# A recurrent unit whose weights rotate through five pairs of buffers in place of three

## The chip, the cores and the metric

The kernel runs on one core of a Trainium2 chip. The metric is the time of one execution in microseconds (us), measured on the device. TensorE is called PE, VectorE DVE, ScalarE ACT, GpSimd POOL and SyncE SP, as in the profile.

## What is computed

One inference step of two layers for 640 tokens (512 latent, 128 context) of width 1024: neighbourhood attention and an FFN, then a gated linear recurrent unit and an FFN. The change is in the recurrent unit:

```python
def _lru_mixer(xm, h0, w_in, conv_w, conv_b, w_a, b_a, w_i, b_i, lam, w_out):
    gate, xr = jnp.split(xm @ w_in, 2, axis=-1)
    xc = _centred_depthwise_conv(xr, conv_w, conv_b)             # width 4
    a_f, b_f = _rglru_coeffs(xc, w_a[0], b_a[0], w_i[0], b_i[0], lam[0])
    a_b, b_b = _rglru_coeffs(xc, w_a[1], b_a[1], w_i[1], b_i[1], lam[1])
    hs_f, hT_f = _linear_scan(a_f, b_f, h0[:, 0], reverse=False)
    hs_b, hT_b = _linear_scan(a_b, b_b, h0[:, 1], reverse=True)
    y = (hs_f + hs_b) * jax.nn.gelu(gate)
    return y @ w_out, jnp.stack([hT_f, hT_b], axis=1)
# _rglru_coeffs: r, i = sigmoid(block-diagonal products of xc); a = exp(-8 r softplus(-lam))
#                b = sqrt(1 - a*a) * i * xc
```

## The kernel before

Features lie on the 128 partitions and tokens along the row; a feature block is 128 features, of which there are eight. A matrix product in fp32 is made of three products in a reduced format: a weight tile of 128 x 1024 elements (one output block, 512 KB) is split into a high part and the low rest, the input likewise, and PE does high x high, high x low and low x high (lines L221 to L223).

`unit` loads one such weight tile. SP fetches `raw` (three buffers). In the recurrent stage POOL fetches the same tile a second time straight into the high part `whi` (L178); in the other stages ACT casts it from `raw` (L180). DVE subtracts (`wlo` = `raw` - `whi`, L182). `whi` and `wlo` have three buffers each, so the fourth tile waits until PE has finished with the first. In both FFN stages a second set, `whx` and `wlx`, takes turns with them (tags in the stage's own pool, three buffers each at most); in the recurrent stage all 16 tiles of `w_in` go through the three pairs.

The recurrent stage runs over t = 0 to 9 as a pipeline of four parts for the eight blocks:
- `lru_xr(f)`: product for the branch `xr` in two pieces of 384 and 256 tokens (tiles `mm`), copied out by ACT (L1251).
- `lru_a`: convolution `xc`, a first step on ACT (L1259) and three on DVE (L1261); four gate products on PE (`gp`, L1271, two PSUM buffers), each read by ACT with a tanh (L1272); an elementwise step on DVE (L1273).
- `lru_b`: exponentials, tanh and square root on ACT (L1283 to L1285), DVE steps L1279, L1286, L1287.
- `lru_c`, `lru_d`: scans on DVE (L1296), POOL copies of a last column to `st` (L1298), sums (L1303, L1304), the product with the GeLU gate (L1308) and the split into high and low (ACT L1313, DVE L1315). `lru_gate` makes the gate's product and its GeLU.

The order in which each engine does its instructions is set when the kernel is built: a scheduler with its own model of durations places them, and each engine then works strictly in that order. Number of buffers and code together therefore decide the queues. Around the end of the stage the output product `project_halves` begins, with three output tiles accumulated over blocks 0 to 5 first and over 6 and 7 when these are ready. Its weights (`in_wlo`) are cast by ACT into `whi` and `whx`.

Of the kernel before, what the change touches and what calls it, by code (L numbers as in the profile page):

```python
# [10 lines left out]
F32R = mybir.dt.float32r  # L11
# [4 lines left out]
P = 128  # L16
# [109 lines left out]
class _Step:  # L126
# [33 lines left out]
        return self.t([P, KT, NTOK + 2], dt, "big", 4)[:, :, 0:n]  # L160


    def unit(self, src, slot=None, after=None):
        nc = self.nc
        _, a, b = src.shape
        raw = self.t([P, a, b], F32, "raw", 3)
        nc.sync.dma_start(raw, src)
        if slot is None:
            self.nu += 1
            slot = "x" if self.wx and self.nu % 2 == 0 else "m"  # L170
        if slot == "x":
            hi = self.t([P, a, b], F32R, "whx", 3, self.sb)
            lo = self.t([P, a, b], F32R, "wlx", 3, self.sb)
        else:
            hi = self.t([P, a, b], F32R, "whi", 3)
            lo = self.t([P, a, b], F32R, "wlo", 3)
        if self.ptags == ["at"]:
            nc.gpsimd.dma_start(hi, src)  # L178
        else:
            nc.scalar.copy(hi, raw)  # L180
        with self.tc.issue_after(after) if after else nullcontext():
            nc.vector.tensor_tensor(lo, raw, hi.bitcast(F32), ALU.subtract)  # L182
        return hi, lo
# [1052 lines left out]
        nc.vector.tensor_scalar(self.hb, self.cols[:, c:c + 4 * KT], 0.5, None, ALU.mult)  # L1236

    def halves(self, w, hi, lo, ev, after=None):
        u = self.unit(w, None, after)
        return [lambda t0=t0, t1=t1, **kw: ev(t0, self.chunk(u, hi, lo, t0, t1, **kw)) for t0, t1 in CHL]  # L1240

    def lru_xr(self, f, hi, lo, after=None):
# [95 lines left out]
    def run(self):  # L1338
# [83 lines left out]
        ylo = self.big()  # L1422
        with self.phase("lru", at=1) as lp:
            A, B, C, G = {}, {}, {}, {}
            self.xrs = [self.t([P, 648], F32, f"xr{j}", 1, lp) for j in range(2)]
            for xr in self.xrs:
                for a, b in ((0, 2), (514, 517), (645, 648)):
                    nc.gpsimd.memset(xr[:, a:b], 0.0)

            def gate(g, after=None):  # L1430
                G[g], halves = self.lru_gate(g, xhi, xlo, lp, after)
                return halves
            x0, g0, x1 = self.lru_xr(0, xhi, xlo), gate(0, self.sq), self.lru_xr(1, xhi, xlo, self.dg)
            x0[0](pins={3: self.at})
            g0[0](pins={0: self.rr})
            for step in (x1[0], x0[1], g0[1]):
                step()
            for t in range(KT + 2):
                if t < KT:
                    A[t] = self.lru_a(t, lp)  # L1440
                if t + 1 < KT:
                    for step in self.lru_xr(t + 1, xhi, xlo) if t else x1[1:]:
                        step()
                if 0 < t <= KT:
                    B[t - 1] = self.lru_b(t - 1, *A.pop(t - 1))
                if t > 1:
                    C[t - 2] = self.lru_c(t - 2, *B.pop(t - 2))
                if t > 2:
                    for step in gate(t - 2):
                        step()  # L1450
                if t > 1:
                    self.lru_d(t - 2, C.pop(t - 2), G.pop(t - 2), yhi, ylo)
            nc.gpsimd.dma_start(o["nh"], self.st)
# [34 lines left out]
```

## Time and profile before

| | us |
|---|---|
| median of the runs | 1523.04 (1518.65, 1523.07, 1523.04) |
| profiled execution, time | 1522.37 |
| profiled execution, span | 1520.6 |
| recurrent stage in the span | about 858 to 1024 |
| PE busy | 1491.2 |
| DVE busy | 1061.5 |
| ACT busy | 698.1 |
| POOL busy | 261.4 |

The span is the part between the first and the last instruction of the profile; times in timelines are from its start. Durations of neighbouring instructions overlap somewhat on PE, DVE and ACT, since they are pipelined, so that a step's cost in a solid stretch is the difference of two starts. "Waited for" names the releaser that the profile infers from semaphores.

### The profile page before, as it was taken

How to read it: one execution, taken by the hardware profiler on the slowest of the kernel's cores; microseconds unless marked ns; L12 is line 12 of the kernel's file. 1: busy time of each engine (PE TensorE's matmuls, PEld its weight loads, DVE VectorE, ACT ScalarE, POOL GpSimd, SP SyncE). 2: the span in 40 equal slices, each digit the busy share in tenths (PEclk: the TensorE clock that was granted, in tenths of full speed). 3: DMA queues.
4: the chain of work that ended last, by engine and by line, in shares of the span. 5: the costliest groups of instructions: out<-in, count | busy, mean ns of one | idle time of the engine just before them, and what ended most of it. 6: DMA issues, size and time to landing. Idle time of an engine off the chain costs nothing. (4 is left out here: it accounts for less than half of the span.)

```text
span 1520.6 us, 26116 instructions
## 1 busy us (share of the span) xinstructions
PE 1491.2 (98%) x10373; PEld 1441.8 (95%) x10373; DVE 1061.5 (70%) x2005; ACT 698.1 (46%) x1268; POOL 261.4 (17%) x276
## 2 busy tenths in 40 slices
PE   8999999999999999999999999899999999999997
PEld 5999999889999999999999887799999999999997
DVE  5778998679999997434443769876975655566555
ACT  4676766654332123312321478764644342434243
POOL 0112132100111110000000014230232323222211
PEclk9999999999999999999999999999999999999999
DMA  9644665446556664222222543316242231323211
GB/s 375 174 143 160 186 189 167 117 139 194 176 185 195 207 196 132 62 84 84 65 73 83 150 134 102 119 59 216 70 156 80 74 111 57 100 67 97 71 56 70
DMA packets 72330, 196.65 MB, mean 129 GB/s; under 512 B 8048, under 2 KB 24592, under 8 KB 72080
## 3 DMA queue, kind: packets, MB, share of 16 engines
q1 hardware_dynamic: 57392, 142.32, 29.6%
q0 software_dynamic: 14240, 51.98, 11.1%
q8 instruction: 81, 1.33, 0.4%
q10 hardware_dynamic: 576, 0.68, 0.1%
q14 instruction: 41, 0.34, 0.1%
HBM read 179.48 MB, written 8.92 MB: 124 GB/s over the span
## 5 line engine op out<-in xcount | busy, mean ns | idle before, releaser
L221 PE MATMUL mm<-big,whi 128*128 128x320 f32 (+3 forms) x1233 | 383.9, 313 | 4.0 <-ACT big L1313 2.8
L222 PE MATMUL mm<-big,whi 128*128 128x320 f32 (+3 forms) x1233 | 384.2, 312 | 1.7 <-DVE big L1315 1.3
L223 PE MATMUL mm<-big,wlo 128*128 128x320 f32 (+3 forms) x1233 | 384.1, 312 | 0.2 <-DVE wlo L182 0.2
L221 PEld LDWEIGHTS mm<-big,whi 128*128 128x128 f32 x1233 | 233.0, 189 | 6.7 <-ACT big L1313 3.5
L222 PEld LDWEIGHTS mm<-big,whi 128*128 128x128 f32 x1233 | 233.6, 189 | 3.8 <-DVE big L1315 2.2
L223 PEld LDWEIGHTS mm<-big,wlo 128*128 128x128 f32 x1233 | 233.2, 189 | 1.6 <-DVE wlo L182 0.4
L250 DVE SCALAR_TENSOR_TENSOR mprod<-mraw,csb 128x1024 f32<-128x1024 f32 x160 | 194.9, 1218 | 11.8 <-DMA mraw<-in_wm 11.4
L590 DVE SCALAR_TENSOR_TENSOR x<-mm,G,x 128x320 f32<-128x320 f32 (+2 forms) x192 | 77.8, 435 | 82.4 <-PE mm L223 82.3
L180 ACT CAST whi<-raw 128x1024 fp32r<-128x1024 f32 (+1 forms) x71 | 73.9, 1041 | 113.9 <-PE mm L222 65.6
L182 DVE TENSOR_TENSOR wlo<-raw,whi 128x1024 fp32r<-128x1024 f32 (+1 forms) x87 | 105.9, 1218 | 28.7 <-ACT whi L180 16.5
L221 PE MATMUL mm<-big,whx 128*128 128x320 f32 (+3 forms) x348 | 108.4, 311 | 0.0
L223 PE MATMUL mm<-big,wlx 128*128 128x320 f32 (+3 forms) x348 | 108.0, 310 | 0.0
L222 PE MATMUL mm<-big,whx 128*128 128x320 f32 (+3 forms) x348 | 107.9, 310 | 0.0
L246 POOL DMA_DIRECT2D mraw<-in_wm x80 | 43.0, 537 | 358.6 <-DVE mprod L250 266.0
L221 PE MATMUL mx<-big,whi 128*128 128x320 f32 (+3 forms) x287 | 89.5, 312 | 0.0
L223 PE MATMUL mx<-big,wlo 128*128 128x320 f32 (+3 forms) x287 | 88.9, 310 | 0.0
L222 PE MATMUL mx<-big,whi 128*128 128x320 f32 (+3 forms) x287 | 88.7, 309 | 0.0
L221 PE MATMUL mx<-big,whx 128*128 128x320 f32 (+3 forms) x260 | 80.6, 310 | 0.0
L223 PE MATMUL mx<-big,wlx 128*128 128x320 f32 (+3 forms) x260 | 80.5, 310 | 0.0
L180 ACT CAST whx<-raw 128x1024 fp32r<-128x1024 f32 (+1 forms) x40 | 41.1, 1029 | 85.9 <-PE mm L222 47.3
L222 PE MATMUL mx<-big,whx 128*128 128x320 f32 (+3 forms) x260 | 80.3, 309 | 0.0
L1313 ACT CAST whi<-raw 128x1024 fp32r<-128x1024 f32 (+1 forms) x41 | 41.3, 1008 | 70.3 <-PE mm L222 45.2
(347 smaller groups left out, 3725.3 us busy)
## 6 DMA issues: line engine op xcount, KB each, us to landing
raw<-in_gu SPq DMA_DIRECT2D x88, 512.0 KB, 3.5
mraw<-in_wm POOLq DMA_DIRECT2D x80, 512.0 KB, 3.9
raw<-in_dn SPq DMA_DIRECT2D x24, 512.0 KB, 3.6
sw<-in_wm SPq DMA_DIRECT2D x16, 512.0 KB, 10.7
raw<-in_wqk SPq DMA_DIRECT2D x16, 512.0 KB, 4.8
raw<-in_wi SPq DMA_DIRECT2D x16, 512.0 KB, 3.5
whi<-in_wi POOLq DMA_DIRECT2D x16, 512.0 KB, 3.9
raw<-in_dn SPq DMA_DIRECT2D x16, 448.0 KB, 3.3
```

Of the source, the lines that this page charges most:

```text
L180: nc.scalar.copy(hi, raw)
L182: nc.vector.tensor_tensor(lo, raw, hi.bitcast(F32), ALU.subtract)
L221: nc.tensor.matmul(ps, hi[:, k], xhi[:, k, s], start=(k == 0), stop=False)
L222: nc.tensor.matmul(ps, hi[:, k], xlo[:, k, s], start=False, stop=False)
L223: self.done = nc.tensor.matmul(ps, lo[:, k], xhi[:, k, s], start=False, stop=(k == last)).ins
L246: nc.gpsimd.dma_start(w, self.i["wm"][l * 6 + j - 2, f])
L250: nc.vector.scalar_tensor_tensor(prod, w, 1.0, self.csb[:, s], ALU.mult, ALU.mult, accum_out=out[:, s, f:f + 1])
L590: self.nc.vector.scalar_tensor_tensor(xs, ps[:, a - t0:b - t0], G[:, s, f:f + 1], xs, ALU.mult, ALU.add)
L1313: self.nc.scalar.copy(hi, v)
```

## The change

The tiles of `w_in` are counted (`lu`, 1 to 16 in the order of the calls). Tiles 6, 8, 11, 13 and 16 use a second set, `whx` and `wlx`, with two buffers in the recurrent stage's own pool; the other eleven stay with the three old pairs. Two pairs of 2 x 4 KB per partition are added. The number of `raw` buffers stays three. From line 1239 on, a line of the kernel after reads one higher than before, and from 1426 on two higher.

```diff
-    def unit(self, src, slot=None, after=None):
+    def unit(self, src, slot=None, after=None, nx=3):
...
         if slot == "x":
-            hi = self.t([P, a, b], F32R, "whx", 3, self.sb)
-            lo = self.t([P, a, b], F32R, "wlx", 3, self.sb)
+            hi = self.t([P, a, b], F32R, "whx", nx, self.sb)
+            lo = self.t([P, a, b], F32R, "wlx", nx, self.sb)
...
     def halves(self, w, hi, lo, ev, after=None):
-        u = self.unit(w, None, after)
+        self.lu += 1
+        u = self.unit(w, "x" if self.lu > 4 and self.lu % 5 in (1, 3) else "m", after, 2)
         return [lambda t0=t0, t1=t1, **kw: ev(t0, self.chunk(u, hi, lo, t0, t1, **kw)) for t0, t1 in CHL]
...
         with self.phase("lru", at=1) as lp:
             A, B, C, G = {}, {}, {}, {}
+            self.lu = 0
```

The scheduler places the instructions anew. Three places follow; numbers in names count tiles, so that a name means the same in both kernels (`whx_10793` and `whi_10793` are the same weight tile in another buffer).

POOL in the middle of the stage, before, weight tiles 12 to 16 and the copies of last columns between them:

```order
L1298 COPY st_74<-lt_9826 128x1 x2
L178 DMA whi_10454<-in_wi 128x1024
L1298 COPY st_74<-lt_9933 128x1
L178 DMA whi_10533<-in_wi 128x1024
L1298 COPY st_74<-lt_9933 128x1
L178 DMA whi_10640<-in_wi 128x1024
L1298 COPY st_74<-lt_10100 128x1 x2
L178 DMA whi_10721<-in_wi 128x1024
L178 DMA whi_10793<-in_wi 128x1024
```

The same copies on POOL after:

```order
L1299 COPY st_74<-lt_9826 128x1 x2
L178 DMA whi_10640<-in_wi 128x1024
L1299 COPY st_74<-lt_9933 128x1
L178 DMA whi_10721<-in_wi 128x1024
L1299 COPY st_74<-lt_9933 128x1
L178 DMA whx_10793<-in_wi 128x1024
L1299 COPY st_74<-lt_10100 128x1 x2
```

Each place between two copies holds a weight tile two further on, and none is left behind the copies of `lt_10100`.

DVE at the last block's convolution (`xc_10595`), before; `wlo_10722` is the low part of tile 15:

```order
L1303 TENSOR_TENSOR lt_10345<-lt_10100 128x448
L1279 TENSOR_SCALAR lt_10433<-lt_10433 128x1286
L1304 TENSOR_TENSOR lt_10345<-lt_10100 128x128
L1261 SCALAR_TENSOR_TENSOR xc_10595<-xr_1598_9510,cols_61,xc_10595 128x643 x2
L182 TENSOR_TENSOR wlo_10722<-raw_10719,whi_10721 128x1024
L1261 SCALAR_TENSOR_TENSOR xc_10595<-xr_1598_9510,cols_61,xc_10595 128x643
L1273 SCALAR_TENSOR_TENSOR lt_10434<-lt_10434,xc_10428 128x1286
```

DVE at the same place after; `wlo_10876` is the low part of the first output weight:

```order
L1304 TENSOR_TENSOR lt_10345<-lt_10100 128x448
L1280 TENSOR_SCALAR lt_10433<-lt_10433 128x1286
L1305 TENSOR_TENSOR lt_10345<-lt_10100 128x128
L182 TENSOR_TENSOR wlo_10876<-raw_10873,whi_10875 128x1024
L1262 SCALAR_TENSOR_TENSOR xc_10595<-xr_1598_9510,cols_61,xc_10595 128x643 x3
L1274 SCALAR_TENSOR_TENSOR lt_10434<-lt_10434,xc_10428 128x1286
```

The output weight's subtraction came here from behind the elementwise step of block 7 (`lt_10601`, L1273), and tile 15's went to the place ahead of the convolution of block 6 (`xc_10428`), where tile 13's stood.

ACT near 898 us, before, at the square root of block 0 (`lt_9677`) and the gate products of block 2 (`gp_9827`, `gp_9831`):

```order
L1272 ACTIVATE lt_9825<-gp_9827,l_hb_2016 128x643
L1285 ACT_TABLE_LOAD
L1285 ACTIVATE lt_9677<-lt_9677 128x1286
L1259 ACTIVATE xc_9927<-xr_1598_9510,cols_61 128x643
L1272 ACT_TABLE_LOAD
L1272 ACTIVATE lt_9825<-gp_9831,l_hb_2016 128x643
```

ACT at the same place after:

```order
L1286 ACT_TABLE_LOAD
L1286 ACTIVATE lt_9677<-lt_9677 128x1286
L1273 ACT_TABLE_LOAD
L1273 ACTIVATE lt_9825<-gp_9827,l_hb_2016 128x643
L1260 ACTIVATE xc_9927<-xr_1598_9510,cols_61 128x643
L1273 ACTIVATE lt_9825<-gp_9831,l_hb_2016 128x643
```

The tanh of `gp_9827` moved behind the square root and both table loads, and the first convolution step of block 3 (`xc_9927`) stays behind both.

## Prediction

> **What bounds the kernel now.** I read the page's busy times first, then the waits of TensorE (PE), then the recurrent stage in stretches, then its timelines. The page's line for the engines (busy us, share of the span, instructions):
>
> ```profile
> span 1520.6 us, 26116 instructions
> PE 1491.2 (98%) x10373; PEld 1441.8 (95%) x10373; DVE 1061.5 (70%) x2005; ACT 698.1 (46%) x1268; POOL 261.4 (17%) x276
> ```
>
> PE idles 29 us in the whole execution, and the change removes no matmul, so only PE's waits and its clock can give time back. PE's waits between 840 and 1060 us (total, times, longest):
>
> ```profile
> PE gp L1271 <- ACT lt L1285: 2.2, 1, 2.2
> PE gp L1271 <- ACT lt L1272: 1.9, 1, 1.9
> PE gp L1271 <- DVE xc L1261: 1.7, 1, 1.7
> PE mm L221 <- ACT big L1313: 1.6, 1, 1.6
> PE mm L223 <- DVE wlo L182: 0.2, 1, 0.2
> ```
>
> The direct wait for a weight is 0.2 us. The four larger ones, which I call A (1.9), B (1.7), C (2.2) and the closing wait T (1.6), are for gate products, convolution and outputs, so weight buffers can help only through the queues of the engines that make these. The stage in stretches (busy us of PE, PEld, DVE, ACT, POOL; granted clock; DMA):
>
> ```profile
> 907.00:917.70 10.70, 8.84 (x53) 7.68 (x52) 10.70 (x14) 9.85 (x14) 9.20 (x3) 1.00 0.27 75
> 917.70:921.20 3.50, 3.50 (x10) 2.47 (x10) 3.50 (x5) 1.80 (x3) 3.50 (x1) 0.51 0.45 147
> 921.20:960.00 38.80, 38.68 (x232) 34.09 (x232) 33.33 (x41) 34.97 (x49) 12.21 (x12) 1.00 0.37 116
> 960.00:982.60 22.60, 18.70 (x109) 15.96 (x108) 19.71 (x23) 18.13 (x25) 4.81 (x4) 1.00 0.39 110
> 982.60:986.00 3.40, 3.40 (x10) 2.29 (x9) 3.37 (x4) 1.71 (x3) 0.00 (x0) 0.50 0.52 202
> 986.00:1022.00 36.00, 35.83 (x237) 34.49 (x236) 27.74 (x34) 23.56 (x31) 10.51 (x6) 1.00 0.17 49
> ```
>
> Behind A and behind C PE runs some 3.4 us at half clock, which costs 1.7 us each beside the wait. In 907 to 917.7 DVE never rests; it sets A.
>
> **Wait C.** Timelines around it (start, length, engine, work, in brackets the idle time before):
>
> ```profile
> 974.91 1.81 DVE L1261 SCALAR_TENSOR_TENSOR xc<-xr,cols,xc 128x643 f32<-128x643 f32 x2
> 979.57 1.23 DVE L182 TENSOR_TENSOR wlo<-raw,whi 128x1024 fp32r<-128x1024 f32 x1 [2.85 <-PE mm L223]
> 980.71 0.88 DVE L1261 SCALAR_TENSOR_TENSOR xc<-xr,cols,xc 128x643 f32<-128x643 f32 x1
> 973.05 2.79 POOL L1298 COPY st<-lt 128x1 f32<-128x1 f32 x1 [0.47 <-DVE lt L1296]
> 975.78 0.53 POOL L178 DMA_DIRECT2D whi<-in_wi  x1
> 981.70 3.75 PE L1271 MATMUL gp<-xc,gw 128*128 128x512 f32 x8 [2.16 <-ACT lt L1285]
> whi<-in_wi POOLq DMA_DIRECT2D x16, 512.0 KB, 3.9
> ```
>
> The trace names the square root (L1285) as C's releaser, but PE starts 0.11 us after the third convolution step (980.71 + 0.88), which the products read: that is what it waited for. In DVE's queue the subtraction for whi_10721 stands between the second and the third step; its weight is issued by POOL at 975.78, behind a one-column copy that takes 2.79 us, and lands 3.9 us later, at 979.7. So a weight that PE needs only some 15 us later holds the convolution.
>
> With the change that weight's subtraction stands 20 us earlier, and here stands the one for the first output weight (wlo_10876), cast by ACT with no POOL DMA. The cast needs the buffer that the products of mm_10485 leave, and these end where ACT copies their result:
>
> ```profile
> 970.35 0.49 ACT L1251 COPY xr<-mm 128x128 f32<-128x128 f32 x2 [0.94 <-PE mm L223]
> 999.74 1.04 ACT L180 CAST whi<-raw 128x1024 fp32r<-128x1024 f32 x1
> 983.41 0.80 ACT L1272 ACTIVATE lt<-gp,l_hb 128x643 f32<-128x643 f32 x1 [0.40 <-PE gp L1271]
> ```
>
> The cast runs at 970.4 to 971.4, long before DVE asks at 975.0. DVE then does 1.14 us of subtraction and three steps of 0.9 (1.81 over two): ready near 978.9 where it was 981.59. PE comes at 981.70 - 2.16 = 979.54, so C goes. With it goes, in this execution, the half-clock stretch. Price on ACT: everything behind 970.35 slides by 1.04. It was ready for the next tanh at 983.01 (983.41 less 0.40 idle) and will be near 984.6 with A's slip added; that tanh ends at 985.4, which is when PE's next product would want its bank (982.2 after the two products, plus 18 matmuls of 0.175). No new PE wait over half a microsecond. PE's lead behind C: 2.16 + 1.7 - 0.5 (the slip of A, below) = 3.4 us.
>
> **Wait B stays.** It has the same cause:
>
> ```profile
> 952.16 3.52 POOL L1298 COPY st<-lt 128x1 f32<-128x1 f32 x1 [10.99 <-DVE lt L1296]
> 955.62 0.53 POOL L178 DMA_DIRECT2D whi<-in_wi  x1
> 959.47 1.23 DVE L182 TENSOR_TENSOR wlo<-raw,whi 128x1024 fp32r<-128x1024 f32 x1 [3.83 <-PE mm L223]
> ```
>
> The new order has another weight there (whi_10721 in place of whi_10533), still behind the same copy on POOL and still ahead of the convolution on DVE: the 3.83 us of DVE and the 1.7 us of PE remain. Gain 0.
>
> **Wait A grows.** ACT takes a tanh out of its place: before, it ran ahead of a square root, now behind it and behind two table loads.
>
> ```profile
> 898.08 0.79 ACT L1272 ACTIVATE lt<-gp,l_hb 128x643 f32<-128x643 f32 x1
> 898.89 1.28 ACT L1285 ACT_TABLE_LOAD   x1
> 900.18 1.28 ACT L1285 ACTIVATE lt<-lt 128x1286 f32<-128x1286 f32 x1
> 902.91 0.88 DVE L1261 SCALAR_TENSOR_TENSOR xc<-xr,cols,xc 128x643 f32<-128x643 f32 x1
> 917.48 2.29 PE L1271 MATMUL gp<-xc,gw 128*128 128x512 f32 x4 [1.86 <-ACT lt L1272]
> ```
>
> Load, root and load from 898.09 end at 902.0, the tanh at 902.7, and the convolution's first step on ACT (0.9) at 903.6; DVE takes it up 0.7 us later than 902.91. DVE has no rest until 917.7 to absorb that, so A's end slips by 0.7; two more matmuls now stand ahead of it (0.24). Net +0.45. One ACT table load more in the stage (22 for 21) falls into the gap that ACT has behind 917.43 and is hidden. In 921 to 960 PE waits 0.12 us of 38.8, DVE and ACT rest 5.5 and 3.8: the slip is carried, not grown. DVE also waits longer for whi_10454 near 926 (up to 1.6 where it waited 0.4); the 1.2 us that it rests at 932 take that up.
>
> **Early weights.** Two extra pairs cost two POOL issues at 852 and 863, and their subtractions move to 863 and 878. PE waits for nothing in 860 to 900, so they cost nothing while whi_9751 (issued behind them) still lands by 871. Subtractions, casts and bytes keep their number.
>
> **The close.** What ends the stage is the chain through the last two outputs, not PE:
>
> ```profile
> 990.04 0.80 ACT L1272 ACTIVATE lt<-gp,l_hb 128x643 f32<-128x643 f32 x1 [2.60 <-PE gp L1271]
> 1004.20 2.45 ACT L1285 ACTIVATE lt<-lt 128x1286 f32<-128x1286 f32 x2
> 1019.00 1.21 DVE L182 TENSOR_TENSOR wlo<-raw,whi 128x1024 fp32r<-128x1024 f32 x1
> 1023.69 1.46 ACT L1313 CAST big<-lt 128x640 fp32r<-128x640 f32 x2 [10.99 <-DVE lt L1308]
> 1024.47 0.41 PE L221 MATMUL mm<-big,whi 128*128 128x320 f32 x1 [1.57 <-ACT big L1313]
> ```
>
> The tanh at 990.04 waits for PE; with PE 3.4 earlier it runs at 986.9, behind two other ACT steps: 3.2 gained. The exponentials then wait some 0.7 for DVE, which now does an output's low part ahead of the scans: the roots come 2.45 earlier than 1004.20. From there DVE is solid, and the subtraction at 1019.00 (1.14 net of overlap) has moved out of that stretch: the cast comes 3.6 earlier. PE, 3.4 earlier, still waits 1.4 for it. In the last pass PE's matmuls now stand tile by tile and no longer interleaved by what is ready: two waits of about 0.2 more for low parts. Gain at the stage's end 3.2 us; behind it PE is solid, and the gain is kept.
>
> **Sum.** C's wait and half clock -3.85; A +0.45; the close +0.2: -3.2. The profiled execution took 1522.37 us, the median of the runs is 1523.04, 0.67 above it. So 1519.2 for an execution like the profiled one, **1519.8** against the median.
>
> **A rule weighed.** The gap of 2.16 us is followed by a clock of 0.50, the gap of 1.86 by 0.51, while the gaps of 1.7 (B) and 1.6 (T) are followed by 1.00. The Trainium skill (TensorE: Matmul & The Clock Gate, Why this matters for your kernels) says that gaps between matmuls should stay under about 3 us, a window of idleness being what halves the clock. By that rule no gap here costs clock and the sum would be -1.5, 1521.5; the trace does not agree, two gaps of about 2 us did cost it. The same page (Part 1) has the window free-running, which no single execution here can show.
>
> **Rivals.**
> 1. The half clock is chance. Gaps of 1.6 and 1.7 us went free, those of 1.9 and 2.2 did not, and one run shown is 4.4 us below the other two, about 2.6 such costs. If the runs of before mostly had no half clock behind C, only 3.2 - 1.7 = 1.5 us are gained: 1521.5.
> 2. More goes: B too, if the copy on POOL happens to get through early. Then 1.7 more, or A's half clock is missed: 1518.1.
> 3. The change does not do what it says: the cast or the table loads ahead of the last convolution come so late that C stays. That needs 978.9 to become 981.6, 2.7 us of slip on ACT or DVE. A's +0.45 and the +0.2 of the last pass would be left, less the 1.14 at the close: -0.5, 1522.5.
> 4. Slower: the weight that DVE now wants near 914.7 (whx_10366) is issued between two copies on POOL:
>
> ```profile
> 908.40 1.00 POOL L1298 COPY st<-lt 128x1 f32<-128x1 f32 x1 [12.88 <-DVE lt L1296]
> 910.03 12.52 POOL L1298 COPY st<-lt 128x1 f32<-128x1 f32 x1
> 906.65 1.28 DVE L1296 TENSOR_TENSOR_SCAN lt<-lt,cols,lt 128x512 f32<-128x512 f32 x1
> ```
>
> The first copy fits into the scans (1.00 us); the second missed them and took 12.52. If A's slip of 0.7 lets the first miss them too, it frees itself only when DVE stops at 914.7; the weight then lands at 914.7 + 0.2 + 3.9 = 918.8, DVE loses 4.1 us where it is the bound, and PE most of that and a further half clock: 5.8 - 3.2 = +2.6, 1525.6. It decides if the first copy starts less than its 1.0 us ahead of the scans' end; I see 1.2.
>
> By the Trainium skill (GPSIMD Engine Reference, Key points) POOL contends with DVE instructions that read two inputs from SBUF, as scans do; then the first copy would be held as well and rival 4 would be the forecast, 1525.6. The row of 1.00 inside the scans speaks against it.
>
> **Chances.** Forecast 0.45 (within 1517.8 to 1521.3), rival 1 0.20, rival 2 0.15, rival 3 0.11, rival 4 0.09. About 0.3% (4.6 us) is what a measurement can tell from no change. Faster by more, below 1518.5: rival 2's most, and the forecast's lower part (0.45 x 0.45), 0.34. Slower by more, above 1527.6: rival 4 together with C staying, 0.08. The rest, 0.58. The range leaves out the far ends of rivals 2 and 4: 1516.0 to 1523.8.
>
> **What would show it.** Right: no PE wait at about 980 and clock 1.00 in the 6 us behind it; the DVE wait of about 3.8 us ahead of 960 and B still there; A between 2 and 2.5 us; a wait at the stage's end of 1 to 1.5 us for the cast. Wrong: a PE wait over 1 us between 978 and 990 (rival 3), DVE idle some 4 us near 915 (rival 4), half clock in a new place, or PE waiting for a weight near 871.

## The result, and the profile after

The changed kernel took 1524.17 us (median of 12 runs, 1518.21 to 1525.75) beside 1521.32 us of the kernel before (12 runs): ratio 1.0026, 95% interval 1.0014 to 1.0037. The forecast was 1519.8, with a range up to 1523.8. A second comparison gave 1523.66 beside 1520.37, ratio 1.0012, 0.9995 to 1.0029. (The ratios compare whole sets of runs and not the two medians, so they can differ from the quotient of the medians.) So by the first comparison the change costs 0.1 to 0.4%, where some 0.2% were to be gained; the second agrees with that, but does not exclude that it costs nothing. The profiled execution of the changed kernel took 1525.75 us, 1.6 over its median.

The page's span and engines after, and two stretches (busy us of PE, PEld, DVE, ACT, POOL; granted clock; DMA):

```profile
span 1524.0 us, 26113 instructions
PE 1492.0 (98%) x10373; PEld 1442.6 (95%) x10373; DVE 1062.5 (70%) x2005; ACT 699.0 (46%) x1269; POOL 264.0 (17%) x276
968.33:971.75 3.42, 3.10 (x5) 1.61 (x6) 3.42 (x4) 1.95 (x4) 0.00 (x0) 0.50 0.00 0
971.75:985.00 13.25, 13.25 (x81) 11.40 (x80) 11.06 (x15) 11.60 (x16) 4.15 (x2) 1.00 0.26 81
```

PE's timeline after, the rows of the recurrent stage ahead of which PE was idle (start, length, work, in brackets the idle time before and its releaser):

```profile
903.44 1.35 PE L1272 MATMUL gp<-xc,gw 128*128 128x512 f32 x4 [0.78 <-ACT lt L1273]
918.72 1.35 PE L1272 MATMUL gp<-xc,gw 128*128 128x512 f32 x4 [1.88 <-ACT lt L1273]
933.04 1.35 PE L1272 MATMUL gp<-xc,gw 128*128 128x512 f32 x4 [1.23 <-ACT lt L1273]
946.26 2.40 PE L1272 MATMUL gp<-xc,gw 128*128 128x512 f32 x8 [0.32 <-issue]
968.65 3.95 PE L1272 MATMUL gp<-xc,gw 128*128 128x512 f32 x8 [3.30 <-DVE xc L1262]
1003.50 0.44 PE L221 MATMUL mm<-big,whx 128*128 128x384 f32 x1 [0.44 <-ACT gl L1326]
1024.33 0.41 PE L221 MATMUL mm<-big,whi 128*128 128x320 f32 x1 [0.73 <-ACT big L1314]
1025.19 0.41 PE L222 MATMUL mm<-big,whi 128*128 128x320 f32 x1 [0.45 <-DVE big L1316]
```

C is gone: no wait near 980, and the clock is 1.00 from 971.75 to 985. But B, which was to stay at 1.74, is 3.30 and has a half-clock stretch of its own at 968.33, and there are new waits at 903, 933 and 946. Measured between the same matmuls of PE, the stage from 842 to 1048 us took 0.16 us less than before: what C and the half clock behind A, absent this time, gave, B with its half clock and the new waits took back.

The 3.4 us between the two profiled spans lie elsewhere. Up to the stage the changed kernel was 0.58 us behind, from half-clock stretches near the start, and between 1085 and 1130 it lost 2.75 more. There a weight landed late (waits of that part, before first, then after):

```profile
ACT wuh L1313 <- DMA raw<-in_gu: 0.8, 1, 0.8
ACT wuh L1314 <- DMA raw<-in_gu: 2.0, 1, 2.0
PE mm L1142 <- DVE g L1104: 1.8, 1, 1.8
```

PE waited 1.8 us where it had waited 0.5, with one more half-clock stretch. No instruction of that part changed its place, and the same wait was 1.58 and 1.30 us in two more profiles of the kernel before, and 1.16 and 1.32 us in two more of the changed kernel. The 0.5 us was the exception: this is chance, and one pair of profiles does not tell what the change did.

### The profile page after: what moved, and what is told of

Same layout as the page of the kernel before. It is cut to its first block, busy times and chain, and to the rows that moved or that the text cites. A ratio compares the mean times of both kernels' runs of the same rounds, so it can differ in the third digit from the quotient of the medians.

```text
span 1524.0 us, 26113 instructions
## 1 busy us (share of the span) xinstructions
PE 1492.0 (98%) x10373; PEld 1442.6 (95%) x10373; DVE 1062.5 (70%) x2005; ACT 699.0 (46%) x1269; POOL 264.0 (17%) x276
## 5 line engine op out<-in xcount | busy, mean ns | idle before, releaser
L221 PE MATMUL mm<-big,whi 128*128 128x320 f32 (+3 forms) x1153 | 358.6, 313 | 3.0 <-ACT big L1314 2.0
L222 PE MATMUL mm<-big,whi 128*128 128x320 f32 (+3 forms) x1153 | 358.8, 312 | 2.0 <-DVE big L1316 1.8
L223 PE MATMUL mm<-big,wlo 128*128 128x320 f32 (+3 forms) x1153 | 358.1, 312 | 0.0
L221 PEld LDWEIGHTS mm<-big,whi 128*128 128x128 f32 x1153 | 217.5, 189 | 5.6 <-ACT big L1314 2.7
L222 PEld LDWEIGHTS mm<-big,whi 128*128 128x128 f32 x1153 | 218.2, 189 | 4.1 <-DVE big L1316 2.4
L223 PEld LDWEIGHTS mm<-big,wlo 128*128 128x128 f32 x1153 | 217.6, 189 | 1.0
L221 PE MATMUL mm<-big,whx 128*128 128x320 f32 (+3 forms) x428 | 133.7, 312 | 0.5 <-ACT gl L1326 0.4
L223 PE MATMUL mm<-big,wlx 128*128 128x320 f32 (+3 forms) x428 | 133.1, 311 | 0.0
L222 PE MATMUL mm<-big,whx 128*128 128x320 f32 (+3 forms) x428 | 132.8, 310 | 0.0
L180 ACT CAST whi<-raw 128x1024 fp32r<-128x1024 f32 (+1 forms) x71 | 73.9, 1040 | 114.5 <-PE mm L222 66.4
L221 PEld LDWEIGHTS mm<-big,whx 128*128 128x128 f32 x428 | 80.6, 188 | 1.1 <-ACT gl L1326 0.7
L222 PEld LDWEIGHTS mm<-big,whx 128*128 128x128 f32 x428 | 80.9, 189 | 0.0
L223 PEld LDWEIGHTS mm<-big,wlx 128*128 128x128 f32 x428 | 80.7, 188 | 0.0
L221 PE MATMUL mx<-big,whx 128*128 128x320 f32 (+3 forms) x260 | 80.6, 310 | 0.0
```

The costliest lines, as they stand in the source:

```text
L221: nc.tensor.matmul(ps, hi[:, k], xhi[:, k, s], start=(k == 0), stop=False)
L222: nc.tensor.matmul(ps, hi[:, k], xlo[:, k, s], start=False, stop=False)
L223: self.done = nc.tensor.matmul(ps, lo[:, k], xhi[:, k, s], start=False, stop=(k == last)).ins
```

## The experiments

The first theory, P, came from POOL's and DVE's timelines after, around 911 to 962:

```profile
911.20 12.66 POOL L1299 COPY st<-lt 128x1 f32<-128x1 f32 x1
923.80 0.53 POOL L178 DMA_DIRECT2D whi<-in_wi  x1
927.75 1.23 DVE L182 TENSOR_TENSOR wlo<-raw,whi 128x1024 fp32r<-128x1024 f32 x1 [1.60 <-issue]
938.49 11.27 POOL L1299 COPY st<-lt 128x1 f32<-128x1 f32 x2 [7.37 <-ACT lt L1284]
949.70 0.53 POOL L178 DMA_DIRECT2D whi<-in_wi  x1
953.65 1.23 DVE L182 TENSOR_TENSOR wlo<-raw,whi 128x1024 fp32r<-128x1024 f32 x1 [3.94 <-issue]
957.25 1.02 POOL L1299 COPY st<-lt 128x1 f32<-128x1 f32 x1 [7.03 <-DVE lt L1297]
958.22 0.53 POOL L178 DMA_DIRECT2D whi<-in_wi  x1
962.16 1.23 DVE L182 TENSOR_TENSOR wlo<-raw,whi 128x1024 fp32r<-128x1024 f32 x1 [1.39 <-issue]
```

The three weights are whi_10454, whi_10640 and whi_10721. The second copy of block 2 (`lt_9826`; 9.78 of the 11.27 us) ended when DVE came to rest at 949.7, and DVE rested because it wanted whi_10640, which POOL issues behind that copy: each held the other. The next copy then came later, and with it whi_10721. Two rivals: Q, that the order on ACT and DVE makes the waits whatever POOL does; R, that the loss is chance outside the stage.

**The changed kernel again**, unaltered.

> The changed kernel once more, unaltered, timed and profiled again. Theory P (the copies hold POOL's queue): with the change the weight of tile 14 (whi_10640) came to stand behind the second copy of the last state of block 2, which took 9.78 us where its counterpart took 1.03; VectorE waited 3.94 us and then 1.39 us for weights and wait B grew from 1.74 to 3.27 us. It is fixed by the order, so it comes again: a copy of 9 to 10 us near 940, B at 3.1 to 3.4 us, ratio to the kernel before 1.0015 to 1.0035. Rival R (chance outside the stage): in the profiled pair the stage itself took 0.16 us less than before and the loss of 2.75 us lay at 1090 to 1115, behind one weight that landed 1.2 us late. Then that place is back at a wait of 0.5 us, and the ratio is 0.9995 to 1.001.

Measured: 1523.66 us (1515.63 to 1525.45, 12 runs). Its profile is of an execution of 1515.63 us (POOL, then PE):

```profile
908.59 6.75 POOL L1299 COPY st<-lt 128x1 f32<-128x1 f32 x1
935.85 3.20 POOL L1299 COPY st<-lt 128x1 f32<-128x1 f32 x1 [0.47 <-DVE lt L1297]
900.83 1.35 PE L1272 MATMUL gp<-xc,gw 128*128 128x512 f32 x4 [0.78 <-ACT lt L1273]
916.13 2.14 PE L1272 MATMUL gp<-xc,gw 128*128 128x512 f32 x4 [1.89 <-ACT lt L1273]
```

The same program, and the two copies took 6.75 and 3.20 us in place of 12.66 and 9.78. B is gone; the stage took 4.5 us less than in the first profile of before. The waits at 933 and 946 are absent too, but for another reason: here a half clock follows A, and PE, some 1.7 us later from there on, meets its products ready. The stretch behind A and the one that follows it, in this profile and then in the first one after:

```profile
916.50:919.90 3.40, 3.40 (x9) 2.09 (x8) 3.40 (x5) 3.35 (x6) 0.00 (x0) 0.51 0.62 190
919.90:960.00 40.10, 40.10 (x242) 36.02 (x241) 37.62 (x45) 36.38 (x48) 13.54 (x10) 1.00 0.43 119
918.70:922.10 3.40, 3.38 (x15) 2.43 (x16) 3.40 (x4) 3.37 (x5) 3.40 (x1) 1.00 0.16 66
922.10:960.00 37.90, 36.35 (x219) 32.03 (x218) 32.37 (x40) 33.96 (x47) 18.22 (x11) 1.00 0.37 106
```

P had said that B is fixed by the order: wrong, the copies' lengths differ between executions of one program, in an order that stays the same. R was wrong as well, since the stage itself differs by 4.3 us between two executions. What the 25 timed executions of the changed kernel show fits that: 5 at 1515.6 to 1518.8, 20 at 1521.1 to 1525.8, none between. The 87 of the kernel before, in this comparison and the later ones, have no such gap (33 below 1519, 24 from 1519 to 1521, 30 above).

**The copies on VectorE**, first in the changed kernel, then in the one before.

```diff
-            nc.gpsimd.tensor_copy(st, h[:, d, e:e + 1])
+            nc.vector.tensor_copy(st, h[:, d, e:e + 1])
```

> The changed kernel with the 16 one-column copies of the last states on VectorE in place of POOL, so that nothing stands ahead of a weight on POOL's queue. Theory P: VectorE's waits for weights near 950 and 961 (3.94 and 1.39 us) fall below 0.5 us together, B falls from 3.27 to under 1 us, and the time falls by 2.3 to 5 us against the changed kernel: ratio to before 0.9985 to 1.0008. Rival Q (the growth comes from ScalarE's order, a tanh behind a square root and one more table load, and from the order on VectorE): B stays above 2.5 us, ratio 1.0015 to 1.003.

> The kernel before with the same copies on VectorE, and three pairs of buffers as it had. Theory P: waits B (1.74 us) and C (2.16 us) both came from weights behind these copies and go; with them goes a half-clock stretch of 1.7 us where it followed C: 3.5 to 5.6 us less, ratio 0.9963 to 0.998. Rival Q (the buffers come free too late, whatever stands on POOL): B and C stay above 1.4 us each, ratio 0.9995 to 1.0005.

Measured: 1524.77 us, ratio 1.0031 (1.0019 to 1.0043), and 1525.73 us, ratio 1.0033 (1.0019 to 1.0047). Both slower, against P. PE's longest wait in the stage, of each:

```profile
PE mm L221 <- ACT big L1314: 6.0, 1, 6.0
PE mm L221 <- ACT big L1313: 8.0, 1, 8.0
```

B and C are at 0.83 us or less in both, as P says, but a wait of 6 to 8 us for the last output's cast stands at the stage's end, with 6.8 us of half clock. Beside the copies themselves the edit moved some two dozen or more instructions each on DVE and ACT and over 150 matmuls on PE, so these two runs mix two changes. They do not decide.

**Two early pairs alone.**

```diff
-        u = self.unit(w, "x" if self.lu > 4 and self.lu % 5 in (1, 3) else "m", after, 2)
+        u = self.unit(w, "x" if self.lu in (6, 8) else "m", after, 2)
```

> Only tiles 6 and 8 take the extra pairs; 11, 13 and 16 go back to the three main pairs. The tanh behind the square root near 902 belongs to this half, the weights of the second half again change their places among POOL's copies. Theory P: the early half costs under 0.7 us by itself, and the time is decided by the copies ahead of tiles 12 to 15 near 940 to 980; ratio 0.999 to 1.0015. Rival Q (ScalarE's order): A at 1.9 to 2.5 us and the new waits of 0.8 and 1.2 us near 903 and 930 come with it, ratio 1.0015 to 1.003.

Measured: 1523.37 us, ratio 1.0016 (1.0001 to 1.003), just inside Q's range and just above P's, with an interval that reaches into both. Its profile has the 0.77 us near 903, so that wait belongs to the early half; it has waits of 2.41 and 2.15 us for a tanh near 932 and 991, the second in no other kernel: another order again. Inconclusive on the time.

**The states by a DMA on POOL's own queue**: now the weights stand behind an issue that does not copy. For the changed kernel the order on PE, ACT, DVE and SP is the same, instruction for instruction; for the one before, one convolution step on DVE moves.

```diff
-            nc.gpsimd.tensor_copy(st, h[:, d, e:e + 1])
+            nc.gpsimd.dma_start(st, h[:, d, e:e + 1])
```

> The changed kernel with the 16 last states written by a DMA on POOL's queue in place of a POOL copy; the order on every other engine is the same, instruction for instruction. Theory P2 (a lottery): the second copy of a pair is starved by VectorE for 1 to 12.7 us, differently in each execution of the same program (12.66 us and 6.75 us for the same copy in two profiles of the changed kernel), and decides whether wait B is 0 or 3.3 us; the changed kernel's executions fall into a group at 1515 to 1519 us and a larger one at 1521 to 1526 for that reason. Without copies the slow group goes: median 1515 to 1518.5, B below 0.5 us, no wait near 934, ratio to before 0.9965 to 0.999. Rival Q (order on ScalarE and VectorE): two groups as before, median 1522 to 1525, ratio 1.001 to 1.003.

> The same edit on the kernel before (one convolution step on VectorE moves, all else keeps its order). P2: B (1.74 us) and C (2.16 us) go, with one half-clock stretch: median 1515 to 1518.5, ratio 0.996 to 0.999. If the two kernels then differ, that is what the buffers alone are worth: P2 says within 1.5 us of one another. Rival Q: B and C stay, ratio 0.9995 to 1.0005, and the changed kernel with this edit is 2 to 4 us slower than this one.

Measured: 1517.15 us (1515.25 to 1521.51), ratio 0.9991 (0.998 to 1.0002), and 1517.59 us (1516.23 to 1518.91), ratio 0.9988 (0.9978 to 0.9998). POOL's rows in the changed kernel with this edit, where the copies of blocks 0 and 2 had been, then DVE's first wait for a weight behind 900, then PE's waits in the stage for a tanh and at the close (total, times, longest):

```profile
910.33 0.54 POOL L1299 DMA_DIRECT2D st<-lt  x1 [0.41 <-issue]
937.49 0.53 POOL L1299 DMA_DIRECT2D st<-lt  x1 [0.96 <-ACT lt L1285]
955.13 1.22 DVE L182 TENSOR_TENSOR wlo<-raw,whi 128x1024 fp32r<-128x1024 f32 x1 [1.24 <-issue]
PE gp L1272 <- ACT lt L1273: 2.6, 2, 1.9
PE mm L221 <- ACT big L1314: 0.7, 1, 0.7
```

No state takes over 0.55 us, B is gone, and but for one run at 1521.51 none is above 1519.9. By the medians that is 6.5 to 7 us less than the changed kernel, which was timed in other comparisons; by the ratios to the kernel before, each within its own comparison, it is 3 to 5 us less. In the kernel before the same edit takes C away and leaves 0.49 of B, in a profile without a half clock behind A:

```profile
963.53 1.78 PE L1271 MATMUL gp<-xc,gw 128*128 128x512 f32 x5 [0.49 <-DVE xc L1261]
PE mm L221 <- ACT big L1313: 1.6, 1, 1.6
```

With the copies out of the way the two kernels differ by 0.4 us in the median, by 0.2 the other way in the mean (1517.9 and 1517.7), and by 0.1 us in the stage of their profiles. With 12 runs each, such differences are within the noise. The five pairs by themselves are worth nothing that these runs can show, and what the change cost goes, as far as they can tell, through the copies. P2 is borne out on B in the changed kernel and on both medians. The changed kernel's ratio is just above P2's 0.999, with an interval that reaches 1.0002, and the absent wait near 934 proves nothing here, since this profile has a half clock behind A.

**The kernel before, profiled twice more.**

> The kernel before, profiled again, to see what of its first profile repeats. P2: wait A (1.86 us) repeats within 0.1 us, since no POOL copy has a part in it; B and C change with the lengths of the copies (3.52 and 2.79 us in the first profile) and lie between 0 and 3 us. Rival: A, B and C all repeat within 0.2 us, and only the half-clock stretches move.

> The same once more, for a third profile of the kernel before: P2 expects one of the three to be without C or without B, the rival expects none.

Measured: 1523.10 and 1518.87 us. PE's waits from 895 to 990, of the first and of the second:

```profile
PE gp L1271 <- ACT lt L1272: 2.5, 3, 1.9
PE gp L1271 <- ACT lt L1285: 2.4, 1, 2.4
PE gp L1271 <- DVE xc L1261: 1.8, 1, 1.8
PE gp L1271 <- ACT lt L1272: 2.4, 2, 1.9
PE gp L1271 <- ACT lt L1285: 1.7, 1, 1.7
PE gp L1271 <- DVE xc L1261: 1.6, 1, 1.6
```

Here P2 missed and its rival was nearer: A, B and C are in all three profiles (1.9, 1.6 to 1.8, 1.7 to 2.4). The kernel before varies too, but in another place: the second copy of block 0 took 12.52, 12.54 and 6.60 us, and DVE waited at most 0.4 us for its weight either way. The second copy of block 2, which took 9.78 and 3.20 us after, took 1.03 in all three: there it met a weight's subtraction on DVE and ended with it, where after the change it met a convolution step. In the first profile of before (POOL):

```profile
939.67 1.03 POOL L1298 COPY st<-lt 128x1 f32<-128x1 f32 x1 [0.47 <-DVE lt L1296]
```

What does change from profile to profile before is the half clock: two stretches in the stage, one, and none.

**One block at a time**, to see which copy does it: `f` is the block.

```diff
-            nc.gpsimd.tensor_copy(st, h[:, d, e:e + 1])
+            (nc.gpsimd.dma_start if f == 0 else nc.gpsimd.tensor_copy)(st, h[:, d, e:e + 1])
```

> The changed kernel with only the two last states of block 0 written by DMA; the other 14 stay POOL copies, and no other engine's order moves. In the slow profile of the changed kernel block 0's second copy took 12.66 us, whi_10454 behind it came late (VectorE waited 1.60, PE 1.23 us near 934), and then block 2's second copy took 9.78 us and B 3.30; in the fast profile the two took 6.75 and 3.20 us and neither wait was there. Theory P3 (the first long copy decides): with block 0 free, block 2's copy takes about 3.2 us in every execution, the slow group is gone, median 1516 to 1519. Rival P4 (block 2's copy is drawn by itself): half or more of the executions stay at 1521 to 1526, median 1520 to 1524.

Measured: 1519.55 us (1515.08 to 1522.56), ratio 1.0002 (0.9989 to 1.0015), some 4 us less than the changed kernel by the medians and 1.5 to 3.6 by the ratios. Block 2's second copy, still a copy, now took what P3 said, and between A and the close PE had no wait over 0.15 us but one of 0.44 for the gate:

```profile
937.25 3.22 POOL L1299 COPY st<-lt 128x1 f32<-128x1 f32 x1 [0.47 <-DVE lt L1297]
```

The median is half a microsecond above P3's range and as much below P4's, and 4 of 12 runs lie at 1521.3 to 1522.6, fewer than P4's half; what they wait for is not in the profile, which is of a run of 1518.56 us.

The same with `f == 2`:

> The same with only the two last states of block 2 written by DMA. Both theories: whi_10640 no longer stands behind a copy that waits for VectorE to rest, so B falls under 0.7 us in every execution. P3: the late whi_10454 remains in part of the executions (PE's 1.23 us near 934), worth 1 to 3 us with a half clock: median 1517 to 1521. Rival P4: block 0's copy costs nothing by itself, median 1516 to 1518.5 as with all 16 moved. Rival Q2: something else holds B, and the slow group at 1521 to 1526 stays.

Measured: 1519.78 us (1516.60 to 1522.51), ratio 1.0006 (0.9994 to 1.0017), in P3's range. Its profile shows both theories wrong on B, and the rival that something else holds B right on that (POOL, DVE, PE):

```profile
910.39 12.71 POOL L1299 COPY st<-lt 128x1 f32<-128x1 f32 x1
927.59 1.23 DVE L182 TENSOR_TENSOR wlo<-raw,whi 128x1024 fp32r<-128x1024 f32 x1 [2.20 <-issue]
952.98 3.58 POOL L1299 COPY st<-lt 128x1 f32<-128x1 f32 x1 [11.72 <-DVE lt L1297]
960.50 1.23 DVE L182 TENSOR_TENSOR wlo<-raw,whi 128x1024 fp32r<-128x1024 f32 x1 [3.99 <-PE mm L223]
967.00 2.43 PE L1272 MATMUL gp<-xc,gw 128*128 128x512 f32 x8 [1.87 <-DVE xc L1262]
```

With block 2 free, block 3's first copy held whi_10721 as it had held whi_10533 before the change (3.52 us of copy, 3.83 of DVE, 1.74 of B): this is the B that the forecast had expected. P3's wait near 933 did not come though DVE waited 2.20 us for whi_10454, since a half clock stood behind A. By the medians each of the two edits takes about 4 us and all 16 copies 6.5 to 7; by the ratios it is 1 to 3.6 us and 3 to 5.

How one copy bears on the next is not shown. That 4 of 12 runs lie above 1521 us with block 0 free, and 20 of 25 of the changed kernel, speaks for block 0's copy as the first step. But the profiles cannot tell it from the clock: block 2's copy was long (9.78 and 9.81 us) where block 0's was long and no half clock stood behind A, and short (3.20 and 3.22) where block 0's was short or a DMA and a half clock stood there. DVE's order beside it is the same in all four.

**The states by SP's queue.**

```diff
-            nc.gpsimd.tensor_copy(st, h[:, d, e:e + 1])
+            nc.sync.dma_start(st, h[:, d, e:e + 1])
```

> The changed kernel with the 16 last states written by SP's queue, so that POOL's queue has the weights alone; the order elsewhere is unaltered. P3 and P4: no copy is starved and no weight waits behind a scan, B and the wait near 934 are 0, median 1514.5 to 1518. Rival: SP's own loads (fp32 weights) now stand behind the scans, PE waits for weights: 1518 to 1523.

Measured: 1517.54 us (1515.30 to 1519.04), ratio 0.9987 (0.9976 to 0.9999). As with POOL's queue, with less spread. This and the kernel before with the DMA are faster than the kernel before by 0.1%, with intervals that just exclude no gain; the changed kernel was slower than the kernel before in its own comparisons.

**A third profile of the changed kernel.**

> A third profile of the changed kernel. P3 and P4 alike: if its time is over 1521 us, the copies of blocks 0 and 2 took over 9 us and B is over 3 us; if it is under 1519 us, they took under 7 us and B is 0. A rival for which the two groups are only half-clock windows: B is over 3 us in both groups.

Measured: 1524.47 us, an execution of the upper group (POOL, PE):

```profile
910.54 12.71 POOL L1299 COPY st<-lt 128x1 f32<-128x1 f32 x1
939.30 9.81 POOL L1299 COPY st<-lt 128x1 f32<-128x1 f32 x1 [0.46 <-ACT lt L1273]
968.30 3.90 PE L1272 MATMUL gp<-xc,gw 128*128 128x512 f32 x8 [3.60 <-DVE xc L1262]
```

As both theories said: copies of over 9 us, B over 3. Three profiles, two kinds of execution, and B follows the copies in each.

## Why the prediction was wrong, point by point

PE's waits in the stage and its half-clock stretches (us; times of the first profile of before):

| near | before | forecast | after, 1525.75 us | after, 1515.63 us | after, states by DMA |
|---|---|---|---|---|---|
| 903 | 0 | 0 | 0.78 | 0.78 | 0.78 |
| A, 917 | 1.86 | 2.31 | 1.88 | 1.89 | 1.87 |
| 933, 946 | 0 | 0 | 1.55 | 0 | 0 |
| B, 966 | 1.74 | 1.74 | 3.30 | 0 | 0 |
| C, 982 | 2.16 | 0 | 0 | 0 | 0 |
| 1003 | 0.17 | 0.17 | 0.44 | 0.44 | 0.38 |
| close, 1024 | 1.57 | 1.4 | 1.18 | 1.17 | 1.18 |
| half-clock stretches | 2 | 1 | 1 | 1 | 1 |

- **Wait C: right.** It was gone in all three profiles of the changed kernel. Its half clock was over-counted: of three profiles of the kernel before, two had a stretch behind C and the third, with a C of 1.67 us, none. Rival 1 had that side.
- **Wait B: this is the step that failed.** The forecast said "Gain 0" because another weight stands behind the same copy of block 3. It looked at whi_10721 alone. The listing in the part on the change shows every gap between two copies with a weight two tiles further on, and whi_10640 had come to stand behind both copies of block 2, with its subtraction ahead of block 3's scans on DVE. The forecast put no price on that. The second of these copies took 1.03 us in the profile that the forecast read; in the changed kernel it took 9.78, 9.81 and 3.20 us, and B came out at 3.30, 3.60 and 0, not at 1.74.
- **Wait A: the place was wrong, the size fair.** The tanh moved behind the root and two table loads did cost, +0.8 for the forecast's +0.45: not at A, which stayed within 0.1 us, but 15 us earlier, where a gate product wanted the bank that this tanh empties (0.78 at 903). That is in every profile of the changed kernel.
- **"921 to 960 is carried": wrong in two of three profiles.** DVE's wait for whi_10454 was 1.60 us as the forecast's bound said, but PE lost 1.2 us near 933 and 0.3 near 946. This wait goes with the clock rather than with the weight: it is there in the two profiles of the changed kernel without a half clock behind A (1.23 and 1.24 us) and absent in the third, which has one, and in its variants by DMA, which have one too; before the change it was 0.44 and 0.51 without one, behind a long copy of block 0 and a short one, and 0 in the first profile, with one. So the forecast erred twice: PE's rows of 921 to 960 were read from an execution whose half clock hid a wait, and a half clock was priced at 1.7 us where, behind A in the changed kernel, most of it comes back.
- **Early weights and the close: nearly right.** At 870 PE waited 0 to 0.76 us for a low part, before 0.24 to 0.41; the close was forecast at 1.4 and took 1.2.
- **The rivals.** Rival 4 had the right mechanism on the wrong weight: it put the trouble at whx_10366 behind the first copy of block 0, which passed in 1.00 us every time; it came with the next copy, and again with block 2's second. Its 1525.6 is at the upper end of the upper group (1521.1 to 1525.8). What the forecast held against it, a copy of 1.00 us inside the scans, was misread: that copy waited too, but only for the end of one scan (last section). Rival 2, that B goes because the copy gets through early, is the lower group (1518.1 forecast, 1515.6 to 1518.8 measured). These are two outcomes of one program, and if the groups follow it as the three profiles do, 20 of 25 executions had the long copies.
- **The rule on gaps under 3 us.** Over the 14 profiles, in the stage and just behind it, all 8 waits of PE between 2.15 and 8.04 us stood beside a half-clock stretch, and 7 of 17 waits of 1.80 to 2.04; four more stretches stood beside waits of 0.7 to 1.75. The Trainium skill (TensorE: Matmul & The Clock Gate, Part 1) has a free-running window of 3413 ns, halved after an idle one; the stretches here are 3.41 us or twice that, but they also follow waits that fill little more than half of such a window, and where the two differ, the measurement decides. So B's growth from 1.7 to 3.3 brought a half clock with it (none stood beside a B of 1.6 to 1.9), and A's comes and goes from one profile to the next. The mean time lost to half clock (span less span times granted clock) was 5.4 us in 87 executions of before and 7.0 in 25 of after: of the 2.9 us between the means, 1.5 are half clock; the rest was not measured apart and would be the waits.

What stays open is why the same copy, beside the same DVE instructions, ends after 6.6 us in one execution and after 12.5 in another, and how block 0's copy, block 2's and the clock behind A depend on one another.

## What to carry to other kernels

When a change moves buffers, look at every queue that an issue shares with other work and write down what now stands ahead of each issue; here the buffers were worth nothing that the runs could show, and replacing the copies that stood ahead gave, by the ratios, some 2 us in the kernel before and 3 to 5 in the changed one. A small instruction that has to wait for another engine's instructions has no length of its own: take its range from several profiles, and ask what lies behind it at the long end. Work that no one waits for, such as these states, belongs on a queue where nothing urgent stands behind it.

## What was not expected of the hardware

Where DVE rested, a 128x1 copy on POOL took 0.20 us. Beside DVE's work it took 0.67 to 12.7 us, and it always ended with a DVE instruction: of the 140 copies in the stage of the nine profiles that have them, all ended within 0.07 us of the end of one, but for five of 0.2 us or less. The usual 1.00 to 1.03 us beside a scan is no free passage either, but what was left of that scan. In the first profile of before, the copy of 1.00 us that the prediction shows at 908.40 ends at 909.40, and the scan that it met ends at 909.42 (first row; the second is a copy while DVE waited):

```profile
908.16 1.26 DVE L1296 TENSOR_TENSOR_SCAN lt<-lt,cols,lt 128x512 f32<-128x512 f32 x1
956.14 0.20 POOL L1298 COPY st<-lt 128x1 f32<-128x1 f32 x1
```

Some copies got in at the first such end and others missed up to 13, until DVE rested or a later end let them in. The same 512 bytes by a DMA issued on POOL took 0.53 to 0.56 us to issue at the same places. The Trainium skill (SBUF — State Buffer, SBUF: two separate sides) has POOL and DVE share a pair of ports as an exclusive lock, which whichever starts first holds for the whole instruction, a DVE operation with two inputs from SBUF among them, while the other is blocked fully. The copies agree with that, those beside scans included.
